# Moving where activation slots and weight tiles begin in SBUF: slots of 4096 bytes at multiples of 512, weights 320 bytes behind one

## The chip, the cores and the metric

One core of a Trainium2 chip. The metric is the device time of one execution in microseconds, the median of several runs; a profile of one further execution shows where its time lies.

## The reference, cut to what matters

Two model blocks follow one another on 256 tokens of width 1024, two layers each, all in float32. A layer of the first block has three attention branches (latent, differential, memory), a gated merge and a feed-forward part; a layer of the second has a state-space branch, a gated recurrence, an mLSTM branch, a merge and a convolved feed-forward part. Most of the work is products with weight matrices:

```python
u = _rmsnorm(h, norm_mix_g[l])
... = _split(u @ w_in[l], IN_SIZES_2)
y_ml = _mlstm_branch(m_q, m_k, m_v, m_i, m_f, m_o, ...)
merged = gate[0] * (y_ssd @ w_br_ssd[l]) + gate[1] * (y_hg @ w_br_hg[l]) + gate[2] * (y_ml @ w_br_ml[l])
h = h + merged @ w_out[l]
up = _dwconv(u @ w_up[l], ffn_conv_w[l], ffn_conv_b[l])
```

In the mLSTM branch the chunk scores are multiplied by the values `v` of each of 8 heads, and by a column of ones, which gives the normalizer.

## The kernel before, in words

**Products.** Each float32 factor is split into a high part of type fp32r and the rest, and a product is three matmuls: high weight by high activation, high weight by low activation, low weight by high activation (`mm` at line 230 issues all of them). `dense_b` (line 238) keeps weights stationary, 128 by 128, and streams 256 tokens of an activation; for each of nk blocks of 128 channels it issues the three, so an output tile is a chain of 3 nk matmuls. `dense_a` (line 262) keeps activations stationary and streams up to 512 columns of weights. `unit` (line 193) brings weights: a DMA of 512 KB into `raw`, a cast to `wh` on ScalarE (line 211), the rest to `wl` on VectorE (line 212). There are 4 `raw`, 6 `wh` and 6 `wl` tiles of 4096 bytes per partition, in pool `wgt`.

**Activations.** `slot` (line 114) hands out one of 24 tiles of `SLOT` = 1040 float32, 4160 bytes, from pool `big`; a block of 128 channels by 256 tokens is 1024 bytes of one. `pair` gives an activation as slots of high parts and slots of low parts, four channel blocks to a slot. Small things live in pools `const` (parameters, tables), `mid` (tiles of 2048 bytes and less, tagged) and `tiny` (32 tiles of 128 bytes).

**Addresses.** Pools lie behind one another in the order in which they are opened (`const`, `wgt`, `big`, `mid`, `tiny`, lines 93 to 97), the first at byte 16512 of each partition; a tile takes its bytes rounded up to 32. By the program's list of tiles the 16 weight tiles begin at 26048, 30144 and so on to 87488, all 448 bytes behind a multiple of 512. The 24 slots begin at 91584 + 4160 s, so slot s lies 448 + 64 s behind one, modulo 512: every multiple of 64 occurs, three times each. Blocks within a tile are steps of 512 or 1024 bytes, so a read has its tile's remainder. Below, the **distance** of an activation is its slot's remainder less the weights' 448, modulo 512. By the same list the activations of the stretches that the prediction reads have these:

| stretch, us | product | distances of high and low parts; after the semicolon those of the other four blocks |
|---|---|---|
| 36 to 50 | `w_in`, first 640 columns, layer 0 | 448 and 384; 64 and 0 |
| 374 to 455 | `mlp_w1`, layer 0 | 0 and 448; 320 and 64 |
| 894 to 966 | `mlp_w1`, layer 1 | 64 and 320; 384 and 256 |
| 1299 to 1327 | `w_br_ssd_2`, layer 0 | 448 and 192; 448 and 448 |
| 1650 to 1726 | `w_up_2`, layer 0 | 64 and 448; 320 and 192 |
| 2244 to 2270 | `w_br_hg_2`, layer 1 | 192 and 192; 0 and 448 |
| 2328 to 2349 | `w_out_2`, layer 1 (stationary) | 192 and 192; 448 and 0 |
| 2356 to 2480 | `w_up_2`, layer 1 | 192 and 64; 256 and 384 |

**Order of the work.** One program order per engine, made by the tile framework from the order of calls; `mix` (line 295) interleaves a stream of products ("main") with a branch's steps ("side") at a given rate, and `high_priority` draws weight loads forward. `ml_cols` (line 1127) takes slots for queries, keys and `va`, the values of four heads and two token halves with a column of ones behind each 128 (2 x 4 x 130 = 1040 floats, the reason for the size of a slot); `dense_a` fills it with one copy per token half; `mlstm` (line 1165) streams `va[:, s, i, :129]` for head i.

Of the kernel before, what the change touches and what calls it, by code (L numbers as in the profile page):

```python
# [9 lines left out]
F32 = mybir.dt.float32  # L10
# [9 lines left out]
P = 128  # L20
# [6 lines left out]
ALPHA = (2 * DEPTH) ** 0.25  # L27
THETA = 500000.0
BIG = 1e30
SLOT = 1040  # L30
AHEAD = 100
DEC = 4
MIX = (1.5, 0.5, 1.3, 1.2, 1.3, 0.9)
# [52 lines left out]
class Kern:  # L86
    def __init__(self, ctx, tc, a, out, dbg=None):
        self.tc, self.nc, self.a, self.out = tc, tc.nc, a, out
        self.dbg = dbg or {}
        nc = tc.nc  # L90
        self.V, self.A, self.T, self.G = nc.vector, nc.scalar, nc.tensor, nc.gpsimd
        pool = lambda n, b, **k: ctx.enter_context(tc.tile_pool(name=n, bufs=b, **k))
        self.pc = pool("const", 1)
        self.pw = pool("wgt", 2)
        self.pb = pool("big", 1)
        self.pm = pool("mid", 2)
        self.pt = pool("tiny", 4)
        self.nslot = 24
        self.fence = []
        self.early = []  # L100
        self.spare, self.turn = True, 0
        self.par = {}
        self.pd = pool("rowd", 1, space=bass.MemoryType.DRAM)
        self.ps = pool("ps", 4, space=PSUM)
        self.evn = 0
        self.nid = 0
        self.consts()
# [31 lines left out]
    def s2(self, shape, dt=F32, bufs=7, tag="s2"):  # L139
        if tag == "s2" and self.spare:  # L140

            self.turn += 1
            if self.turn * DEC // 12 != (self.turn - 1) * DEC // 12:
                return self.shape(self.pm.tile([P, 768], dt, tag="dec", name=self.nm(tag), bufs=DEC), shape)
        n = 512 if tag == "s2" else int(np.prod(shape))
        t = self.pm.tile([P, n], dt, tag=tag, name=self.nm(tag), bufs=bufs)
        return self.shape(t, shape)

    def tiny(self, shape, dt=F32):
        t = self.pt.tile([P, 32], dt, tag="tiny", name=self.nm("tiny"), bufs=32)  # L150
        return self.shape(t, shape)

    def psum(self, tag, shape, bufs):
# [224 lines left out]
    def params(self, vecs, tag):  # L378

        rows = sum(int(np.prod(v.shape)) // P for v in vecs)  # L380
        assert rows <= P
        r = self.pc.tile([P, P], F32, tag="prow", name=self.nm("prow"), bufs=1)
        o, offs = 0, []
        for v in vecs:
            n = int(np.prod(v.shape)) // P
            self.nc.sync.dma_start(out=r[o:o + n], in_=v.rearrange("(n p) -> n p", p=P))
            offs.append((o, n))
            o += n
        ps = self.ptp((P,))
        self.tr(out=ps[:, :rows], in_=r[:rows], identity=self.ident[:rows, :rows])  # L390
        c = self.pc.tile([P, P], F32, tag="pcol" + tag, name=self.nm("pcol"), bufs=2)
        self.V.tensor_copy(out=c[:, :rows], in_=ps[:, :rows])
        return [c[:, o:o + n] for o, n in offs]

# [160 lines left out]
    def first_layer(self, l, x, xT, last, filler):  # L555
        nc, V, A, T, a = self.nc, self.V, self.A, self.T, self.a
        w = a["w_in"][l]
# [12 lines left out]
            V.tensor_tensor(out=lt[:, 2 * i], in0=lt[:, 2 * i], in1=lt[:, 2 * i + 1], op=MUL)  # L570
            V.reduce_sum(out=lr[:, i:i + 1], in_=lt[:, 2 * i], axis=AX.X)
        A.activation(out=lr, in_=lr, func=AF.Exp)
        nlam = self.pc.tile([P, 1], F32, tag="nlam", name=self.nm("nlam"), bufs=2)
        V.tensor_tensor(out=nlam, in0=lr[:, 1:2], in1=lr[:, 0:1], op=SUB)
        V.tensor_scalar(out=nlam, in0=nlam, scalar1=-lam0, scalar2=None, op0=ADD)

# [4 lines left out]
        for i, (k0, k1) in enumerate(((0, 3), (3, 5))):  # L581
# [3 lines left out]
            for tt in range(2):  # L585
                for k in range(k0, k1):
                    self.mm(out=pss[:, 2 * i + tt:2 * i + tt + 1], lhsT=sq[k - k0][:, tt * P:(tt + 1) * P],
                             rhs=self.ones[:, :1], start=k == k0, stop=k == k1 - 1)
        rs = self.pc.tile([P, 4], F32, tag="lrs", name=self.nm("lrs"), bufs=2)
        self.rsqrt(rs[:, :2], pss[:, :2], 1.0 / 384, EPS)  # L590
        self.rsqrt(rs[:, 2:], pss[:, 2:], 1.0 / 256, EPS)
        cq, ck = self.pair(3), self.pair(2)
# [191 lines left out]
        if last:  # L784
            ms = self.s2((2, 2), tag="ms", bufs=2)
# [124 lines left out]
    def second_params(self, l):  # L910
        nc, V, A, a = self.nc, self.V, self.A, self.a
        lb = None
        flat = lambda v: v.rearrange("a b -> (a b)")
        nmix, cw, cbias, sng, hng, mng, nffn = self.params(
            [a["norm_mix_g_2"][l], flat(a["ssd_conv_w_2"][l]), a["ssd_conv_b_2"][l], a["ssd_norm_g_2"][l],
             a["hg_norm_g_2"][l], a["ml_norm_g_2"][l], a["norm_ffn_g_2"][l]], "a")
        fw = a["ffn_conv_w_2"][l]
        cols = [fw[0], fw[1]] + ([flat(a["hg_lb_raw_2"][i]) for i in range(DEPTH)] if l else [])
        f0, f1, *lbr = self.params(cols, "b")
        f2, fb = self.params([fw[2], a["ffn_conv_b_2"][l]], "c")  # L920
        sb = self.pc.tile([P, 96], F32, tag="sbias", name=self.nm("sbias"), bufs=2)
        for o, v in ((0, flat(a["ssd_dt_bias_2"][l])), (32, flat(a["ml_f_bias_2"][l])), (48, flat(a["ml_i_bias_2"][l])),
                     (64, flat(a["ssd_a_log_2"][l]))):
            n = v.shape[0]
            nc.sync.dma_start(out=sb[:, o:o + n], in_=v.rearrange("(o n) -> o n", o=1).broadcast_to([P, n]))
        dsk = self.pc.tile([P, 8], F32, tag="dsk", name=self.nm("dsk"), bufs=2)
        dv_ = a["ssd_d_2"][l].rearrange("(k two) -> two k", two=2)
        for i in range(2):
            nc.sync.dma_start(out=dsk[i * 64:(i + 1) * 64], in_=dv_[i:i + 1].broadcast_to([64, 8]), allow_slow_non_contiguous=True)
        V.tensor_scalar(out=dsk, in0=dsk, scalar1=0.5, scalar2=None, op0=MUL)  # L930
        for g_, c_ in ((sng, 0.5), (hng, 0.25), (mng, 0.5)):
            V.tensor_scalar(out=g_, in0=g_, scalar1=c_, scalar2=None, op0=MUL)
        if l:

            lb = self.pc.tile([P, 4, 16], F32, tag="lb", name=self.nm("lb"), bufs=2)
            mx, e0, e1 = (self.tiny((16,)) for _ in range(3))
            V.tensor_tensor(out=mx, in0=lbr[0], in1=lbr[1], op=MAX)
            for e_, r_ in ((e0, lbr[0]), (e1, lbr[1])):
                V.tensor_tensor(out=e_, in0=r_, in1=mx, op=SUB)
                A.activation(out=e_, in_=e_, func=AF.Exp)  # L940
            V.tensor_tensor(out=mx, in0=e0, in1=e1, op=ADD)
            V.reciprocal(out=mx, in_=mx)
            V.tensor_tensor(out=e0, in0=e0, in1=mx, op=MUL)
            V.tensor_tensor(out=e1, in0=e1, in1=mx, op=MUL)
            V.tensor_tensor(out=e1, in0=e0, in1=e1, op=ADD)
            V.tensor_tensor(out=lb[:, 0], in0=e1, in1=e0, op=SUB)
            V.tensor_scalar(out=lb[:, 1], in0=lb[:, 0], scalar1=-1.0, scalar2=1.0, op0=MUL, op1=ADD)
            V.tensor_scalar(out=lb[:, 2], in0=lb[:, 0], scalar1=0.5, scalar2=0.5, op0=MUL, op1=ADD)
            V.tensor_scalar(out=lb[:, 3], in0=lb[:, 1], scalar1=0.5, scalar2=None, op0=MUL)
        return nmix, cw, cbias, sng, hng, mng, nffn, f0, f1, f2, fb, sb, dsk, lb  # L950

    def second_layer(self, l, h, ms, rest):
        nc, V, A, a = self.nc, self.V, self.A, self.a
        w = a["w_in_2"][l]
        nmix, cw, cbias, sng, hng, mng, nffn, f0, f1, f2, fb, sb, dsk, lb = self.par[l]

        uT = self.rms_ch(h, ms, nmix, rest)
# [19 lines left out]
        ps = self.ptp((2, 64))  # L977
# [20 lines left out]
        dt = self.s2((2, 32), tag="dt", bufs=1)  # L998
# [128 lines left out]
        def ml_cols(hg):  # L1127
            o = 512 * hg
            q, k = self.slot((4, S)), self.slot((4, S))
            va = self.slot((2, 4, 130))  # L1130
            V.memset(va[:, :, :, 128:129], 1.0)
            def gen():
                yield from self.dense_b(uT, w[:, 7712 + o:7712 + o + 512], lambda j, m, ps: self.copy(q[:, j:j + m], ps))
                yield from self.dense_b(uT, w[:, 8736 + o:8736 + o + 512],
                                        lambda j, m, ps: A.mul(out=k[:, j:j + m], in_=ps, mul=128 ** -0.5))
                yield from self.dense_a(uT, [w[:, 9760 + o:9760 + o + 512]],
                                        lambda ci, tt, ps: self.copy(va[:, tt, :, :P], ps.rearrange("p (a b) -> p a b", b=P)))
            return (q, k, va), gen()
        def ml_gate(hg):
            o = 512 * hg  # L1140
# [24 lines left out]
        def mlstm(hg, rows, q, k, va, mo, out):  # L1165
            rd, atok, em = rows
            hs = self.slot((2, 4, P))
            sums = self.s2((2, 2, 4), tag="sums", bufs=2)
            def head(i):
# [9 lines left out]
                for tt in range(2):  # L1179
                    ps = self.ppo((2, 129))  # L1180
                    f = [(e[:, 0, tt * P:(tt + 1) * P], 0)] + ([(e[:, 1, S:], 1)] if tt else [])
                    b = [(e[:, 1, tt * P:(tt + 1) * P], 1)] + ([] if tt else [(e[:, 0, S:], 0)])
                    for d, ops in enumerate((f, b)):
                        for n, (lh, s) in enumerate(ops):
                            self.mm(out=ps[:, d], lhsT=lh, rhs=va[:, s, i, :129], start=n == 0, stop=n == len(ops) - 1)
                    den = self.tiny((2,))
                    A.activation(out=den, in_=ps[:, :, 128], func=AF.Abs)
                    V.tensor_tensor(out=den, in0=den, in1=em[:, tt, :, hd], op=MAX)
# [1 line left out]
                    o = hs[:, tt, i]  # L1190
# [4 lines left out]
            out = out()  # L1195
# [313 lines left out]
```

## Time and profile before

| | us |
|---|---|
| median of 3 runs | 2580.66 |
| the runs | 2576.44, 2580.66, 2670.82 |
| the profiled execution | 2577.26 |
| its span, first to last instruction | 2575.5 |

The runs are whole executions. All rows below belong to the profiled one, whose times run from its span's start. PE is TensorE's matmuls, PEld its weight loads, DVE is VectorE, ACT ScalarE, POOL GpSimd. A matmul's end is modelled and matmuls overlap, so the time of one in a row (0.28 us) is longer than the time from its start to the next one's.

### The profile page before, as it was taken

The numbers are of one execution on the slowest core, as the hardware profiler recorded it, in microseconds if no ns is written. First come the engines' busy times: TensorE is split into PE (matmuls) and PEld (weight loads), VectorE is DVE, ScalarE is ACT, GpSimd is POOL, SyncE is SP. The second block draws the span as 40 slices with busy tenths as digits, with TensorE's granted clock in tenths as the row PEclk, the third lists the DMA queues.
The fourth block names the chain that finished last, engine by engine and source line by source line (L and its number), as shares of the span: only waits on it lengthen the run. The fifth ranks groups of instructions, "written<-read, shape, count | busy, mean of one in ns | idle before, by whom it ended". The sixth has DMA issues, their size and how long they took to land. (4 is left out here: it accounts for less than half of the span.)

```text
span 2575.5 us, 50287 instructions
## 1 busy us (share of the span) xinstructions
PE 2503.5 (97%) x20432; PEld 2294.5 (89%) x20432; DVE 1846.5 (72%) x3229; ACT 1347.5 (52%) x2249; POOL 119.0 (5%) x175
## 2 busy tenths in 40 slices
PE   8999999999999999899899999999999999999998
PEld 8888999888889898798899998998898989998996
DVE  5577686566776865786678877985786689768875
ACT  5455455344654553465654445664556645445653
POOL 0000000000000000013300000000104200000000
PEclk9999999999999999899999999999999999999999
DMA  6643466556434565466564455655567554455653
GB/s 201 198 125 104 148 201 192 190 167 199 127 103 153 173 197 202 137 211 191 165 185 133 134 155 161 205 188 176 165 188 223 156 158 129 147 160 177 188 185 118
DMA packets 352424, 432.37 MB, mean 168 GB/s; under 512 B 21923, under 2 KB 279231, under 8 KB 352191
## 3 DMA queue, kind: packets, MB, share of 16 engines
q1 hardware_dynamic: 347838, 410.12, 51.4%
q0 software_dynamic: 4352, 19.03, 2.4%
q8 instruction: 161, 2.64, 0.4%
q14 instruction: 73, 0.59, 0.1%
HBM read 427.89 MB, written 1.20 MB: 167 GB/s over the span
## 5 line engine op out<-in xcount | busy, mean ns | idle before, releaser
L230 PE MATMUL mm<-s,wh 128*128 128x256 f32 (+1 forms) x8064 | 1464.5, 284 | 1.6 <-DVE s L521 0.7
L230 PEld LDWEIGHTS mm<-s,wh 128*128 128x128 f32 (+1 forms) x8064 | 1242.6, 189 | 19.2 <-issue 13.1
L212 DVE TENSOR_TENSOR wl<-raw,wh 128x1024 fp32r<-128x1024 f32 (+1 forms) x776 | 933.8, 1211 | 436.1 <-ACT wh L211 431.4
L211 ACT CAST wh<-raw 128x1024 fp32r<-128x1024 f32 (+1 forms) x776 | 799.0, 1039 | 770.4 <-PE mm L230 672.5
L230 PE MATMUL mm<-s,wl 128*128 128x256 f32 x4032 | 1136.7, 282 | 0.0
L230 PEld LDWEIGHTS mm<-s,wl 128*128 128x128 f32 x4032 | 761.3, 189 | 3.1 <-issue 2.7
L230 PE MATMUL mm<-wh,s 128*128 128x512 f32 (+2 forms) x2160 | 673.4, 393 | 11.8 <-DVE s L520 6.6
L230 PEld LDWEIGHTS mm<-wh,s 128*128 128x128 f32 x2160 | 406.2, 191 | 102.5 <-DVE s L520 8.4
L230 PE MATMUL mm<-wl,s 128*128 128x512 f32 (+2 forms) x1080 | 421.4, 390 | 0.0
L230 PEld LDWEIGHTS mm<-wl,s 128*128 128x128 f32 x1080 | 206.5, 191 | 43.0
L230 PE MATMUL tp<-s,s 128*32 128x16 f32 (+5 forms) x3552 | 120.7, 208 | 6.7 <-issue 4.5
L233 PE MATMUL tp<-cst,s 128*128 128x128 f32 (+1 forms) x608 | 93.2, 284 | 21.8 <-DVE s L825 6.4
L907 ACT ACTIVATE dec<-dec,rtok 128x256 f32<-128x256 f32 x192 | 73.3, 447 | 74.3 <-POOL dec L903 66.9
L853 DVE SCALAR_TENSOR_TENSOR s<-mm,pcol,s 128x255 f32<-128x255 f32 (+1 forms) x272 | 112.0, 473 | 0.0
L230 PEld LDWEIGHTS tp<-s,s 128*32 128x32 f32 (+3 forms) x3552 | 91.0, 119 | 23.5 <-issue 7.9
L233 PEld LDWEIGHTS tp<-cst,s 128*128 128x128 f32 (+1 forms) x608 | 70.8, 142 | 37.3 <-issue 10.1
L893 POOL DMA_DIRECT2D rds<-rows x8 | 4.1, 518 | 1627.6 <-DVE rows L876 1627.6
L455 ACT ACTIVATE s<-tp,tiny 128x256 f32<-128x256 f32 x112 | 52.1, 471 | 51.7 <-DVE tiny L452 44.9
L1406 DVE TENSOR_TENSOR s<-s,s 128x512 f32<-128x512 f32 x112 | 71.9, 685 | 9.3 <-PE tp L230 8.8
L335 ACT CAST s<-s 128x512 fp32r<-128x512 f32 x46 | 28.3, 619 | 57.3 <-DVE s L765 37.4
L1057 DVE TENSOR_TENSOR dec<-dec,s 128x768 f32<-128x768 f32 x32 | 32.4, 1016 | 35.3 <-ACT dec L907 24.4
L230 PE MATMUL po<-s,s 128*128 128x128 f32 (+2 forms) x352 | 54.0, 311 | 1.1 <-DVE s L344 0.8
(237 smaller groups left out, 1591.1 us busy)
## 6 DMA issues: line engine op xcount, KB each, us to landing
raw<-in_w_in_dram SPq DMA_DIRECT2D x338, 512.0 KB
raw<-in_mlp_w_dram SPq DMA_DIRECT2D x128, 512.0 KB
raw<-in_w_up_dram SPq DMA_DIRECT2D x88, 512.0 KB
raw<-in_w_down_dram SPq DMA_DIRECT2D x44, 512.0 KB
raw<-in_w_branch_dram SPq DMA_DIRECT2D x32, 512.0 KB
raw<-in_w_out_dram SPq DMA_DIRECT2D x32, 512.0 KB
dec<-rds POOLq DMA_DIRECT2D x32, 384.0 KB, 5.4
raw<-in_mem_w_kv_dram SPq DMA_DIRECT2D x16, 512.0 KB
```

Of the source, the lines that this page charges most:

```text
L211: i.append(self.A.copy(out=h, in_=raw))
L212: i.append(self.V.tensor_tensor(out=l, in0=raw, in1=h.bitcast(F32), op=SUB))
L230: return self.T.matmul(**k)
L233: return self.T.transpose(**k)
L335: return (self.A.copy(out=xh, in_=src), self.V.tensor_tensor(out=xl, in0=src, in1=xh.bitcast(F32), op=SUB))
L455: self.A.activation(out=e[:, i], in_=sc[:, i], func=AF.Exp, bias=mx[:, i:i + 1], scale=scale, accum_out=sm[:, i:i + 1])
L853: V.scalar_tensor_tensor(out=o, in0=x, scalar=w[i][c + d], in1=o, op0=MUL, op1=ADD)
L893: self.nc.gpsimd.dma_start(out=d[:, s, c], in_=src)
L907: self.A.activation(out=e[:, s, o], in_=e[:, s, o], func=AF.Exp, scale=-1.0, bias=tok[:, s, q:q + 1])
L1057: V.tensor_tensor(out=e, in0=e, in1=cb[hd // 8], op=MUL)
L1406: V.tensor_tensor(out=xv, in0=xv, in1=tv[:, :, tside].unsqueeze(2).to_broadcast([P, 2 * m, L]), op=MUL)
```

## The change

The pools are opened in another order and a new one, `small`, comes first; `gap` comes between the weights and the slots, and `const` behind the slots. `nlam`, `lrs` and `dsk` move to `small`, `ms` and `sums` to `gap`. A slot has 1024 floats. The values of the mLSTM branch no longer fit one: heads 0 to 2 take a slot, head 3 a tile of tag `va` in pool `mid`, filled by two copies per token half where there was one, and the column of ones by two memsets. To pay for that, `tiny` has 31 tiles and one parameter tile 96 columns.

```diff
-SLOT = 1040
+SLOT = 1024
@@
+        self.pa = pool("small", 1)
+        self.pw = pool("wgt", 2)
+        self.pg = pool("gap", 1)
+        self.pb = pool("big", 1)
         self.pc = pool("const", 1)
-        self.pw = pool("wgt", 2)
-        self.pb = pool("big", 1)
         self.pm = pool("mid", 2)
@@ def s2
-        t = self.pm.tile([P, n], dt, tag=tag, name=self.nm(tag), bufs=bufs)
+        t = (self.pg if tag in ("ms", "sums") else self.pm).tile([P, n], dt, tag=tag, name=self.nm(tag), bufs=bufs)
@@ def tiny
-        t = self.pt.tile([P, 32], dt, tag="tiny", name=self.nm("tiny"), bufs=32)
+        t = self.pt.tile([P, 32], dt, tag="tiny", name=self.nm("tiny"), bufs=31)
@@ def params
-        c = self.pc.tile([P, P], F32, tag="pcol" + tag, ...)
+        c = self.pc.tile([P, 96 if tag == "c" else P], F32, tag="pcol" + tag, ...)
@@ nlam, lrs and dsk, two tiles each
-        nlam = self.pc.tile([P, 1], ...)
+        nlam = self.pa.tile([P, 1], ...)
@@ def ml_cols
-            va = self.slot((2, 4, 130))
-            V.memset(va[:, :, :, 128:129], 1.0)
+            va = self.slot((2, 3, 130)), self.s2((2, 1, 130), tag="va", bufs=2)
+            for t in va:
+                V.memset(t[:, :, :, 128:129], 1.0)
+            def ev_v(ci, tt, ps):
+                ps = ps.rearrange("p (a b) -> p a b", b=P)
+                self.copy(va[0][:, tt, :, :P], ps[:, :3])
+                self.copy(va[1][:, tt, :, :P], ps[:, 3:])
@@
-                                        lambda ci, tt, ps: self.copy(va[:, tt, :, :P], ...))
+                yield from self.dense_a(uT, [w[:, 9760 + o:9760 + o + 512]], ev_v)
@@ def mlstm
-                            self.mm(out=ps[:, d], lhsT=lh, rhs=va[:, s, i, :129], ...)
+                            self.mm(out=ps[:, d], lhsT=lh, rhs=va[i // 3][:, s, i % 3, :129], ...)
```

## Rows read from the trace of the kernel before

**Rows 1.** The page: busy time of two engines; the granted clock in 40 slices.

```profile
PE 2503.5 (97%) x20432; PEld 2294.5 (89%) x20432; DVE 1846.5 (72%) x3229; ACT 1347.5 (52%) x2249; POOL 119.0 (5%) x175
...
PEclk9999999999999999899999999999999999999999
```

**Rows 2.** Matmuls grouped by shape: count, busy us and mean ns, idle before.

```profile
L230 PE MATMUL mm<-s,wh 128*128 128x256 f32 x8032 | 1458.9, 284 | 1.6 <-DVE s L521 0.7 <-DVE s L520 0.6
L230 PE MATMUL mm<-s,wl 128*128 128x256 f32 x4016 | 1132.2, 282 | 0.0
L230 PE MATMUL mm<-wh,s 128*128 128x512 f32 x1984 | 632.9, 399 | 9.5 <-DVE s L520 6.6 <-DVE s L521 1.4 <-ACT wh L211 1.3
L230 PE MATMUL mm<-wl,s 128*128 128x512 f32 x992 | 393.3, 396 | 0.0
```

**Rows 3.** Timeline in `mlp_w1`, layer 0: start us, length us, engine, line, operation, count.

```profile
371.02 0.28 PE L230 MATMUL mm<-s,wh 128*128 128x256 f32 x1
371.02 0.19 PEld L230 LDWEIGHTS mm<-s,wl 128*128 128x128 f32 x1
```

**Rows 4.** Windows of `dense_b` alone, PE: length us, busy us (matmuls), clock, DMA.

```profile
36.50:50.30 13.80, 13.80 (x118) 1.00 0.41 121
893.70:966.20 72.50, 72.50 (x618) 1.00 0.65 202
1650.50:1726.40 75.90, 75.90 (x646) 1.00 0.59 190
2356.00:2480.00 124.00, 124.00 (x1051) 1.00 0.62 195
374.00:455.00 81.00, 81.00 (x702) 1.00 0.66 208
1299.50:1310.00 10.50, 10.50 (x95) 1.00 0.48 147
```

**Rows 5.** Timeline of `w_br_hg_2`, layer 1, on PE, columns as in rows 3.

```profile
2246.06 0.40 PE L230 MATMUL mm<-s,wh 128*128 128x256 f32 x2
...
2247.13 0.40 PE L230 MATMUL mm<-s,wh 128*128 128x256 f32 x2
...
2247.48 0.40 PE L230 MATMUL mm<-s,wh 128*128 128x256 f32 x2
...
2247.83 0.39 PE L230 MATMUL mm<-s,wh 128*128 128x256 f32 x2
...
2248.85 0.40 PE L230 MATMUL mm<-s,wh 128*128 128x256 f32 x2
```

**Rows 6.** Timeline of `w_br_ssd_2`, layer 0, on PE, 1321.8 to 1324.

```profile
1321.82 0.40 PE L230 MATMUL mm<-s,wh 128*128 128x256 f32 x2
...
1323.94 0.28 PE L230 MATMUL mm<-s,wh 128*128 128x256 f32 x1
```

**Rows 7.** Windows of `dense_a` alone, PE, columns as in rows 4.

```profile
467.00:547.90 80.90, 80.90 (x350) 1.00 0.57 185
966.50:1055.00 88.50, 88.50 (x384) 1.00 0.58 188
2327.90:2349.50 21.60, 21.60 (x96) 1.00 0.53 167
```

**Rows 8.** What PE waited for: us in total, times, longest.

```profile
PE tp L230 <- POOL s L1095: 9.4, 4, 3.6
PE mm L230 <- DVE s L520: 7.2, 8, 1.5
...
PE mm L230 <- ACT wh L211: 1.3, 1, 1.3
```

**Rows 9.** Window with the busiest VectorE: PE, PEld, DVE, ACT, POOL, clock, DMA.

```profile
1600.00:1700.00 100.00, 99.37 (x838) 98.69 (x837) 88.91 (x150) 66.10 (x100) 0.00 (x0) 1.00 0.61 191
```

**Rows 10.** Copies of 512 columns from a product's PSUM tile, by engine and shape.

```profile
L344 DVE COPY s<-mm 128x512 f32<-128x512 f32 x26 | 17.8, 686 | 6.1 <-PE mm L230 6.1
...
L346 ACT COPY s<-mm 128x512 f32<-128x512 f32 x26 | 15.1, 582 | 8.4 <-PE mm L230 8.4
```

More of the change, by code (lines that the diff above doesn't have):

```diff
@@ L390, in params @@
         self.tr(out=ps[:, :rows], in_=r[:rows], identity=self.ident[:rows, :rows])
-        c = self.pc.tile([P, P], F32, tag="pcol" + tag, name=self.nm("pcol"), bufs=2)
+        c = self.pc.tile([P, 96 if tag == "c" else P], F32, tag="pcol" + tag, name=self.nm("pcol"), bufs=2)
         self.V.tensor_copy(out=c[:, :rows], in_=ps[:, :rows])
@@ L572, in first_layer @@
         A.activation(out=lr, in_=lr, func=AF.Exp)
-        nlam = self.pc.tile([P, 1], F32, tag="nlam", name=self.nm("nlam"), bufs=2)
+        nlam = self.pa.tile([P, 1], F32, tag="nlam", name=self.nm("nlam"), bufs=2)
         V.tensor_tensor(out=nlam, in0=lr[:, 1:2], in1=lr[:, 0:1], op=SUB)
@@ L588, in first_layer @@
                              rhs=self.ones[:, :1], start=k == k0, stop=k == k1 - 1)
-        rs = self.pc.tile([P, 4], F32, tag="lrs", name=self.nm("lrs"), bufs=2)
+        rs = self.pa.tile([P, 4], F32, tag="lrs", name=self.nm("lrs"), bufs=2)
         self.rsqrt(rs[:, :2], pss[:, :2], 1.0 / 384, EPS)
@@ L925, in second_params @@
             nc.sync.dma_start(out=sb[:, o:o + n], in_=v.rearrange("(o n) -> o n", o=1).broadcast_to([P, n]))
-        dsk = self.pc.tile([P, 8], F32, tag="dsk", name=self.nm("dsk"), bufs=2)
+        dsk = self.pa.tile([P, 8], F32, tag="dsk", name=self.nm("dsk"), bufs=2)
         dv_ = a["ssd_d_2"][l].rearrange("(k two) -> two k", two=2)
@@ L1135, in gen @@
                                         lambda j, m, ps: A.mul(out=k[:, j:j + m], in_=ps, mul=128 ** -0.5))
-                yield from self.dense_a(uT, [w[:, 9760 + o:9760 + o + 512]],
-                                        lambda ci, tt, ps: self.copy(va[:, tt, :, :P], ps.rearrange("p (a b) -> p a b", b=P)))
+                yield from self.dense_a(uT, [w[:, 9760 + o:9760 + o + 512]], ev_v)
             return (q, k, va), gen()
@@ L1184, in head @@
                         for n, (lh, s) in enumerate(ops):
-                            self.mm(out=ps[:, d], lhsT=lh, rhs=va[:, s, i, :129], start=n == 0, stop=n == len(ops) - 1)
+                            self.mm(out=ps[:, d], lhsT=lh, rhs=va[i // 3][:, s, i % 3, :129], start=n == 0, stop=n == len(ops) - 1)
                     den = self.tiny((2,))
```

## The prediction

> **What bounds the kernel now.** First the page: TensorE is busy 97% of the span and its clock is granted in full (2.4 GHz) but for one slice, VectorE 72%, ScalarE 52% [rows 1]. Then who waits: 61 waits of PE in 21 lines, 61.1 us in all, the largest on GpSimd's sum of squares and on the splits that end a norm; on a cast of weights 1.3 us [rows 8]. So the kernel is a stream of matmuls, and the question is how far apart they start. By shape, 12,048 of the 20,432 are 256-column matmuls of `dense_b` and 2,976 are 512-column ones of `dense_a` [rows 2]. While one streams its moving operand, the weight load of the next already runs: both rows begin at 371.02 [rows 3]. The means of rows 2 are modelled and overlap, so spacing is read elsewhere.
>
> In a window of nothing but such matmuls the spacing is its length over the count, less the 2.4 that were in flight at its start (0.28 us each, one every 0.118). That gives 72.5/615.6 = 117.8 ns in `mlp_w1` of layer 1, 75.9/643.6 = 117.9 and 124/1048.6 = 118.3 in the two `w_up`, but 81/699.6 = 115.8 in `mlp_w1` of layer 0 and 10.5/92.6 = 113.4 in `w_br_ssd` of layer 0 [rows 4]. Same shape, same clock; the DMA shares of 0.48 to 0.66 don't order them (0.59 goes with 117.9, 0.66 with 115.8). What does is the table of distances between slots and weight tiles. At 113.4 every slot lies 192 or 448 behind the weights, the same modulo 256. In layer 0's `mlp_w1` half of the blocks (320 and 64, the same modulo 256 again) run at 113.5 in 31 chains and the other half (0 and 448) at 117.7: mean 115.6. Mixed distances stay at 117.5 or more: 117.8 and even in `w_up` of layer 0, where all are odd multiples of 64, and 13.8/115.6 = 119.4 in the slowest window, with 384 beside 448.
>
> The change puts weights at 320 and slots at 0: every distance becomes 192. That case stands in the trace: in `w_br_hg` of layer 1 the first four blocks have 192 and 192, the last 0 and 448. From 2246.06 to 2247.13, nine starts in the last four, (2247.13 - 2246.06)/9 = 119 ns; in the next chain, after an entry of three matmuls, (2248.85 - 2247.83)/9 = 113.3 [rows 5]. All eight half chains of this kind there, three of them after a stall of 0.3 us, settle so within five matmuls (entry gaps 122, 116, 114).
>
> But distance alone doesn't decide. In the same `w_br_ssd` product, after some microseconds at the 1.2 GHz level and back, the same slots run at (1323.94 - 1321.82)/18 = 117.8 [rows 6]. So there are two steady spacings, 113.4 and 117.8, and how a stretch is entered chooses.
>
> **The change part by part.** All is summed against the profiled execution, 2577.26 us (span 2575.5), 3.4 us under the median of the runs.
>
> *Addresses.* Three pairs of small tiles of 32 bytes move `wgt` to 16512 + 192 = 16704 = 32 x 512 + 320. Its 16 tiles of 4096 end at 82240; `ms` (2 x 32) and `sums` (2 x 64) make 82432 = 161 x 512, where slots begin, each a multiple of 512. The distance is 0 - 320 = 192 everywhere.
>
> *`dense_b`.* Of its 12,096 matmuls (48 have 64 columns) 11,707 start less than 140 ns before the next, on average 117.8; the rest follow a stall, another shape or the half clock and keep their time. The stretch of 1299.5 to 1310 with its entry gives 113.6. Gain at full effect: 4.2 x 11,707 = 49 us.
>
> *`dense_a`.* Here weights move and slots are stationary. In flight are 1.7; 80.9/348.3 = 232.3 and 88.5/382.3 = 231.5 with mixed slots, 21.6/94.3 = 229.1 in `w_out` of layer 1, half of whose blocks have 192 [rows 7]. I take 231.5 to 229.0, 2.5 x 2,877 undisturbed = 7 us; the bounds are the slowest window, 232.3 (2 us lost), and the same gain once more, 226.5 (14 us), since only half of that stretch had the new distance.
>
> *What takes some back.* 61 waits of PE [rows 8] end with work of other engines that doesn't hurry. A wait grows by what PE gains since that work was released: at most about a unit of 48 matmuls, 48 x 4.2 = 0.2 us, 12 us for all, 0 where PE's own result was awaited; I take 5. VectorE at its busiest has 88.9 of 100 us [rows 9], 92 at the new pace, no bound. Weights come at up to 202 GB/s in rows 4 and would at 210.
>
> *The state.* Chains at 192 alone went short in 8 of 8 cases; the long state of rows 6 came out of a half-clock stretch, and the page shows few of these. I count a tenth of `dense_b` at 117.8: 5 us; the bounds are none (0) and all (49).
>
> *Values of the mLSTM.* Two layers, two head groups, two token halves: 8 copies of 512 columns become 16, of 384 and 128. A copy costs 0.69 us on VectorE, 0.58 on ScalarE [rows 10]; the added one costs at least nothing, if halves run side by side on two engines, and at most a whole one, 8 x 0.69 = 5.5 us, beside products of 24 x 2 matmuls that last 11 us. I take 0 on the path; without that cover, 3. Four more memsets of 8 columns, parts of a tenth of a microsecond each: 0. One `tiny` fewer of 32 can delay a writer by one reader; no wait in rows 8's view is for such a slot: 0, bound 1. Behind a delayed VectorE write would stand the weight splits, which run ahead by up to six tiles. Tables that only move keep shape and engine: 0; no row shows an address that slows VectorE or ScalarE, and I allow 1 us either way. No DMA is added or moved, and `raw` keeps its shape.
>
> Sum: -49 - 7 + 5 + 5 = -46, so 2577 - 46 = **2531 us**. That is 1.9% under the median, close to the 2% that a measurement of this kernel can tell from no change.
>
> **Against a rule.** Rows 4 to 6 show equal matmuls at two spacings. The Trainium skill ("TensorE: Matmul & The Clock Gate", Part 2, on loading the stationary operand) says that moving operand and weight load have read ports of their own, so that loading the next weights takes nothing from the running matmul. By it addresses can't matter and the time would be 2577; this trace doesn't agree, 113.4 against 117.8 ns. It is a rival below for the part that the trace leaves open.
>
> **The rivals.**
> 1. *All short (0.27).* As above without the long tenth, and waits that grow by 1 or 2 us alone: 2577 - 49 - 7 + 2 = 2523, with 226.5 in `dense_a` 2516. For it: 8 of 8. Against: rows 6. It is faster by over 2% from 2529 down.
> 2. *The long spacing keeps most (0.15).* The state of rows 6 is taken at an entry and kept: `dense_b` 117.8, `dense_a` gains 0 to 7: 2570 to 2577. Half of it as a mixture would be 2548. For: rows 6, and `mlp_w1` of layer 1, where the half at 64 and 320 ran at 117.8 too. Against: those were other distances, but for rows 6. The rule above gives the same time by another way.
> 3. *Slower (0.05).* Slots are now 4096 apart, so high and low parts agree in twelve bits of their address, as no pair before did. If reads of the two in turn collide, the spacing is that of the slowest window, 119.4 [rows 4]: 1.6 x 11,707 = 19, with 2 of `dense_a` 2598. It decides from a mean spacing above 118; over 2% (2632) it takes 122.5, which no window shows.
> 4. *It doesn't do what it says (0.02).* If pools begin at larger steps, distances are equal but another number: 2520 to 2590.
>
> **How the numbers follow.** The forecast, mostly short, has 0.51, its own range 2522 to 2545. Rival 1 has 0.27, 2 has 0.15, 3 has 0.05, 4 has 0.02. The range 2514 to 2574 holds all of the first two, and half of rival 2. Faster by over 2%: rival 1 and a fifth of the forecast, 0.27 + 0.10 = 0.37; slower by over 2%: a fifth of rival 3 and as much for what isn't listed, 0.02; within 2%: 0.61.
>
> **What would show it.** Windows inside `w_up` and `mlp_w1` with 113.4 between starts (75.9 us for 646 matmuls becomes 73), `dense_a` at 229, and PE's waits nearly as long as now. It is wrong if flat 117.8 stands in `w_up`, if the short stretches are there and the waits of PE have grown by 20 us or more, or if spacings differ where all distances are one.

## The result and the profile after

The changed kernel takes 2548.95 us (median of four runs, 2536.19 to 2550.88), the kernel before 2578.55 beside it; the ratio on record is 0.9873, 95% interval 0.9851 to 0.9895 (the two medians alone give 0.9885). One run of the kernel before, 2670.82 us, is a slow one, 3.7% over its fastest, and doesn't count in the ratio. The forecast was 2531 with a range of 2514 to 2574. Measured twice more, unedited, the changed kernel gave 0.9899 [0.9879, 0.9919] and 0.9866 [0.9850, 0.9883]. The gain is 1.0 to 1.3%; by the three pairs of medians it is 24 to 33 us, half to 70% of the 46 us that were forecast. The profiled run took 2536.19 us and is the shortest of all; where a reading hangs on that, other profiles of the same kernel stand beside it.

Busy time and clock of the page, and the two shapes of `dense_b`, which answer to [rows 1, 2] (lines of the kernel after lie some four higher):

```profile
PE 2455.7 (97%) x20432; PEld 2253.2 (89%) x20432; DVE 1850.5 (73%) x3237; ACT 1348.5 (53%) x2253; POOL 117.2 (5%) x175
...
PEclk9999999999999999899999999999999999999999
```

```profile
L234 PE MATMUL mm<-s,wh 128*128 128x256 f32 x8032 | 1418.9, 280 | 2.0 <-DVE s L525 0.7 <-DVE s L524 0.5 <-DVE s L857 0.3
L234 PE MATMUL mm<-s,wl 128*128 128x256 f32 x4016 | 1119.3, 279 | 0.0
```

PE has the same 20,432 matmuls and is as full as before; it only takes 48 us less for them. VectorE and ScalarE have their added instructions (8 and 4) and nearly their old times. So the change lies in the spacing of the matmuls. Windows of nothing but `dense_b`, columns as in [rows 4], in order: the 640-column product of layer 0, `mlp_w1` of layers 0 and 1, `w_up` of layer 0 before and behind the loading of parameters, `w_up` of layer 1:

```profile
37.00:50.80 13.80, 13.80 (x119) 1.00 0.43 121
357.90:449.50 91.60, 91.60 (x811) 1.00 0.62 193
882.70:952.40 69.70, 69.70 (x618) 1.00 0.67 208
1581.20:1626.00 44.80, 44.80 (x383) 1.00 0.68 208
1629.40:1702.40 73.00, 73.00 (x646) 1.00 0.64 196
2319.80:2438.90 119.10, 119.10 (x1053) 1.00 0.66 202
```

Less the 2.4 in flight, that is 118.4, 113.3, 113.2, 117.7, 113.4 and 113.4 ns. `mlp_w1` of layer 1 and both large `w_up` stood at 117.8 to 118.3 before. Every distance is now 192, and still the first and the fourth window are at the long spacing. Below, a stretch at 113.4 is called short and one at 117.8 long; this state is its spacing alone. From the starts of all matmuls in the trace: stretches without an interruption run flat at 113.4 or at 117.8, never between, and a stretch keeps its spacing to its end. That the two are one product is seen in `w_up` of layer 0, where one small transpose changes the state (timeline, columns as in [rows 3]):

```profile
1626.93 0.40 PE L234 MATMUL mm<-s,wh 128*128 128x256 f32 x2
...
1628.70 0.40 PE L234 MATMUL mm<-s,wh 128*128 128x256 f32 x2
...
1629.06 0.24 PE L237 MATMUL tp<-cst,prow 88*128 88x88 f32 x1
```

Ahead of it fifteen starts take (1628.70 - 1626.93)/15 = 118 ns; behind it the window of 1629.4 to 1702.4 above has 113.4, with the same tiles and addresses. In all four profiles of the unedited kernel the state changes at this transpose, in three from long to short and in one the other way. In the kernel moved on by 64 bytes, below, it doesn't: both sides are long.

`dense_a`, 231.5 to 232.3 ns in [rows 7], in the product behind `mlp_w1` of layer 0:

```profile
450.00:541.00 91.00, 91.00 (x399) 1.00 0.59 186
```

Less the 1.7 in flight that is 91/397.3 = 229.0 ns. The mean over all undisturbed `dense_b` matmuls (starts less than 140 ns apart) went from 117.82 to 114.59 ns, of `dense_a` from 231.53 to 229.15: 3.2 x 11,725 = 38 and 2.4 x 2,871 = 7 us. With 5 us more waits of PE (61.1 to 66.3 in sum) that is -40; the two profiled executions differ by 41. The other three profiles of the changed kernel took 2552 to 2557 us; what sets them apart comes below.

### The profile page after: what moved, and what is told of

Same layout as the page of the kernel before. It is cut to its first block, busy times and chain, and to the rows that moved or that the text cites. A ratio compares the mean times of both kernels' runs of the same rounds, so it can differ in the third digit from the quotient of the medians.

```text
span 2533.5 us, 50296 instructions
## 1 busy us (share of the span) xinstructions
PE 2455.7 (97%) x20432; PEld 2253.2 (89%) x20432; DVE 1850.5 (73%) x3237; ACT 1348.5 (53%) x2253; POOL 117.2 (5%) x175
## 5 line engine op out<-in xcount | busy, mean ns | idle before, releaser
L234 PE MATMUL mm<-s,wh 128*128 128x256 f32 (+1 forms) x8064 | 1424.6, 280 | 2.0 <-DVE s L525 0.7
L234 PEld LDWEIGHTS mm<-s,wh 128*128 128x128 f32 (+1 forms) x8064 | 1228.6, 188 | 19.2 <-issue 11.4
L234 PE MATMUL mm<-s,wl 128*128 128x256 f32 x4032 | 1123.8, 279 | 0.0
```

The lines of the kernel that those rows point to most:

```text
L234: return self.T.matmul(**k)
```

## The experiments

Two theories stand at the start. R: the relation of slot and weight addresses allows two spacings, and the state at entry picks one. M: it is the slots' beginning at multiples of 512 that counts. S is the rival by which addresses don't matter and the gain comes from the order of the pools or the split of the values. The Trainium skill ("TensorE: Matmul & The Clock Gate", Part 2), with a read port each for moving operand and weight load, speaks for it. The runs below don't agree (in the kernel 119.9 ns at distance 0 against 114.6 at 192). The first three experiments on the kernel are one execution each, with one of the kernel before beside them (2573.62 us).

### The same distance at other addresses

```
+        self.pa.tile([P, 16], F32, name="pad_small")
         self.pc = pool("const", 1)
```

> Every tile behind the small ones is moved on by 64 bytes: weights 384, slots 64 behind a multiple of 512, distance still 192. Theory R: as the changed kernel, 2531 to 2552 us, the long `w_up` and `mlp_w1` stretches flat at 113.4 ns in most cases. Theory M: slots are no longer at multiples of 512, so 117.8 ns and 2570 to 2580 us. Theory S: 2531 to 2552 us, since pool order and split stay.

Measured: 2549.29 us. Windows in `mlp_w1` of layer 1 and the two `w_up`:

```profile
887.80:960.30 72.50, 72.50 (x618) 1.00 0.68 208
1633.30:1709.20 75.90, 75.90 (x647) 1.00 0.63 190
2333.30:2452.40 119.10, 119.10 (x1053) 1.00 0.66 202
```

Slots at 64 behind a multiple of 512 give the same two spacings: 113.4 in the last window, 117.8 in the first two, which were short in the kernel after. M falls. R's "in most cases" is a miss: `mlp_w1` of both layers and `w_up` of layer 0 behind its transpose are long, and by the mean of 115.16 ns 39% of all `dense_b` matmuls. The state isn't settled by the distance.

### Distance 0 at multiples of 512

```
+        self.pa.tile([P, 48], F32, name="pad_small")
+        self.pg.tile([P, 80], F32, name="pad_gap")
         self.pc = pool("const", 1)
```

(and three of the `tiny` buffers fewer, to make room)

> Weights and slots both begin at multiples of 512, distance 0 everywhere. Theory R: distance 0 gave 117.7 ns in the kernel before (half of `mlp_w1` of layer 0, with 448 beside it), so nearly all of `dense_b` at 117.8 ns and 2570 to 2585 us. Theory M: slots are at multiples of 512, so as the changed kernel, 2531 to 2552 us. Theory S: 2531 to 2552 us.

Measured: 2592.32 us, 19 over the kernel before. Windows in `mlp_w1` of layer 1, in both `w_up`, and in `dense_a`:

```profile
896.30:970.10 73.80, 73.80 (x617) 1.00 0.63 196
1658.10:1735.40 77.30, 77.30 (x647) 1.00 0.60 187
2369.90:2496.10 126.20, 126.20 (x1054) 1.00 0.63 192
974.00:1057.00 83.00, 83.00 (x368) 1.00 0.62 195
```

73.8/614.6 = 120.1 ns in `dense_b`, flat in every stretch (mean 119.87); 83/366.3 = 226.6 in `dense_a`. This falsifies M and S at once: rounder addresses made the kernel slower. It also corrects R, which had expected 117.8. Distance 0 has a spacing of its own, over the mean of every long mixed stretch, and the shortest seen for `dense_a`.

### Mixed distances with the rest of the change

```
-        t = self.pb.tile([P, SLOT], dt, tag="s4", ...
+        t = self.pb.tile([P, SLOT + 16], dt, tag="s4", ...
```

(and twelve `tiny` buffers fewer)

> The changed kernel with slots 4160 bytes apart, so that all eight remainders occur again; weights stay at 320, the values of the mLSTM stay split and the pools keep the new order. Theory R: `dense_b` back at 117.5 to 118 ns, `dense_a` at 231 to 232, 2572 to 2582 us. Theory M: one slot in eight is at a multiple of 512: 2570 to 2580 us. Theory S: the gain stays, 2531 to 2552 us.

Measured: 2580.95 us, `dense_b` at 118.07 and `dense_a` at 231.55 in the mean. The same four places:

```profile
897.10:969.90 72.80, 72.80 (x618) 1.00 0.64 196
1653.80:1729.60 75.80, 75.80 (x646) 1.00 0.61 189
2360.00:2483.80 123.80, 123.80 (x1054) 1.00 0.63 195
588.50:643.70 55.20, 55.20 (x240) 1.00 0.66 198
```

The whole gain is gone. Of the 7 us over the kernel before, 0.25 x 11,700 = 3 are the spacing, and the rest lies within the spread of that kernel's own runs (2573.62 to 2582.81). PE's waits are 63.6 us in sum, against 61.1 before, so the fewer `tiny` buffers hide no gain of size. The split of the mLSTM's values and the new order of the pools bring nothing on their own. S falls.

### The spacing by itself

```
    for d in DIST:                    # 29 distances
        for r in range(6):
            part(1 + r)               # 1 to 6 fp32 matmuls, two passes each
            for i in range(4):
                chain(d, i % 2)       # 12 matmuls: wh,xh  wh,xl  wl,xh
```

> Nothing but matmuls of the two kinds: for each of 29 distances between slots and weights, six chains of 48 `dense_b`-like matmuls (256 columns, a high and a low slot, a high and a low weight tile, in the kernel's order), each entered through one to six fp32 matmuls; then, for 16 distances, three times 24 `dense_a`-like matmuls of 512 columns. The reference's computation is left out. Theory R (the relation of the two addresses and the state at entry set the spacing): the steady spacing is 113.4 or 117.8 ns, at distances 192 and 448 113.4 in most of the six entries, at mixed ones 117.8, and which entries give 117.8 differs with the number of matmuls ahead. Theory M (slots at multiples of 512 bytes decide, whatever the weights): 117.8 at every distance but where slots lie at a multiple of 512, distance 384 here. Theory S (addresses don't matter, the gain came from the pool order and the split of the values): one spacing at all 29 distances.

Windows of single chains of 48: distance 0, then 32, then the first two entries at 192.

```profile
39.50:45.10 5.60, 5.60 (x49) 1.00 0.00 0
57.80:63.30 5.50, 5.50 (x49) 1.00 0.01 3
239.20:244.70 5.50, 5.50 (x49) 1.00 0.01 3
245.30:250.60 5.30, 5.30 (x49) 1.00 0.00 0
```

The same 49 matmuls fill 5.3 us in one entry and 5.5 in the one before it, with next to no DMA and with VectorE and ScalarE idle. The ends of a window cost some tenths of a matmul, so the table is taken from the starts, matmul 7 to 48 of each chain (7 to 24 for 512 columns):

```
distance   256 columns, ns (by entry)    512 columns, ns
0          120.0                         226.7 (some start at 230.8)
32         116.7                         233.3
64         117.8                         233.3
96         120.0                         234.2 to 234.5
128        118.6                         232.3
160        117.3 or 118.6                233.3
192        113.3 or 117.8 (3 of 6 each)  228.8
224        118.3                         233.4
```

256 to 480 repeat this row by row: only the remainder modulo 256 counts. (At 640 and 896, which are like 128, two of the six entries gave 120.0.) R was right at 192 and 448, and too simple elsewhere: not one long spacing, but one or two for each distance. 192, with its like 448, is the only one of these 16 with a spacing under 116; finer steps, below, find another.

### High and low tiles at different remainders, and what picks the state

```
    for d1, d2, e in GRID:      # xh from wh: d1; xl from wl: d2; xl and wl moved on by e
    for n, c, d in SEP:         # n leads of c columns at distance d, then distance 192
```

> Again nothing but matmuls, the reference's computation left out. First chains of 24 `dense_b`-like matmuls over an 8 x 8 table of two distances, of the high slot from the weights that load while it streams, and of the low slot from those that load while it streams, each entered after 2, 4 and 6 passes of fp32; then finer distances around 192, and distance 192 with low slot and low weights moved on together by 32, 64 or 128 bytes. Theory R in its sharper form (each matmul is held up by the weight load of the next one, and only the distance of these two counts): moving both low tiles together changes nothing, 113.3 or 117.8 ns; the diagonal of the table repeats the 29 distances measured before, 0 at 120.0, 32 at 116.7, 192 at 113.3 or 117.8; no pair is under 113.3. Rival: the absolute address counts too, and moving both gives a third spacing. Then distance 192 with one to four extra matmuls ahead of the chain, of another distance or another number of columns: if the state is a phase between the two reads, some of these ends at 113.3 in all six entries; if it is chance, each of them gives about half.

With low slot and low weights moved on together by 32, 64 or 128 bytes every matmul still sees distance 192 from the weights that load meanwhile, and yet the steady spacing is 119.1, 118.4 and 120.9. The sharper form of R falls: where the low tiles begin against the high ones counts as well. In the table of pairs only 192 with 192 reached 113.3 in more than one entry (two of three); one entry at 64 with 64 did too. None is under 113.3. Among the finer distances, 112 has a mean of 114.3 to 114.5 in its three entries (matmul 9 to 24), which the next section takes apart. Of the leads, one of 128 columns at distance 192 and one of 256 at distance 0 or 32 gave 113.3 in six of six entries; without one it was three of six.

### Fifteen ways in

```
    for sep in SEP:                 # none, or a lead
        for kind, n in PRE:         # 15 entries
            pre(kind, n)
            chain2(sep)             # distance 192
```

> Nothing but matmuls, the reference's computation left out. Chains at distance 192 entered in 15 ways (1 to 3 fp32 matmuls of 128, 256 or 64 columns, a 512-column product, a wait for VectorE of four lengths), each plain and with seven leads: a 128-column matmul ahead of the first one (it gave 113.3 in six of six entries before), the first matmul in two halves of 128 columns, in 64 and 192, in 192 and 64, and 128 or 256 columns at another distance. Phase theory (the state is the phase between two periodic reads at entry, so a lead that shifts one of them by a fixed amount picks it): the plain chains split between 113.3 and 117.8, one or two leads give 113.3 in at least 13 of 15. Chance theory: every lead gives about as many as the plain chains. Then distances 96 to 152 in steps of 4, from the 114.4 ns that 112 gave in three of three entries: if 112 is no accident, 108 to 116 lie between 113 and 118, and some distance needs no luck at entry; its 512-column matmuls are 229 to 234.

```
lead ahead of the chain             113.3 ns in, of 15
none                                8
128 columns                         15
256 columns, distance 32            15
first matmul as 128 + 128           14
256 columns, distance 0             13
first matmul as 64 + 192            13
first matmul as 192 + 64            7
128 columns, distance 32            5
```

Not chance: what starts just ahead of the chain picks the state. And 112 is no accident: its mean is 114.2 to 114.5 in four of four entries too, while 108 and 116 have 120 and 122. This mean is no spacing of its own. The first entry, three starts from row to row:

```profile
62.43 0.28 PE L47 MATMUL mm<-sh,wl 128*128 128x256 f32 x1
...
63.49 0.28 PE L47 MATMUL mm<-sh,wl 128*128 128x256 f32 x1
...
64.85 0.28 PE L47 MATMUL mm<-sh,wl 128*128 128x256 f32 x1
```

Nine starts take 1.06 us, 117.8 ns; the twelve behind them 1.36 us, 113.3. So it went in all seven entries at 112, four here and three in the study before: about ten matmuls at 118 to 119, then 113.3 to the end of the 24. At 192 no plain chain left the long state. So 112 may need no luck at entry, as the expectation asked; how it holds over a long stretch wasn't run. Its price is `dense_a`: 512 columns take 233 there against 229 at 192.

### The changed kernel again

> The changed kernel once more, unedited. Theory R: its stretches are flat at 113.4 or 117.8 ns again, but not the same ones as in the first profile; each 4.4 ns x matmuls of the stretches that flip make up the difference of the two times, which is 2536 to 2551 us. Rival (the place in the program sets the state): the same stretches at the same spacing, and a difference of times that comes from waits.

Measured: 2556.41 us, beyond what R had. The mean spacing is 114.72, nearly that of the first profile, and all stretches over 400 matmuls are short in both. States do flip, as R had it: some 2,300 of 11,600 matmuls, short to long for 1,350 and the other way for 980. But that nearly cancels: 0.13 ns x 11,700 = 1.5 of the 20 us between these two runs. The rest is the rival's waits, with the clock beside them. Where they arise is seen by laying the same matmuls of both side by side. Six places are together 19.9 us longer; two of them (columns: length; busy time of PE, PEld, DVE, ACT, POOL; clock; DMA), first profile:

```profile
1209.10:1235.90 26.80, 24.68 (x203) 22.45 (x202) 21.33 (x24) 20.48 (x44) 12.78 (x17) 1.00 0.77 226
...
1944.40:1970.20 25.80, 24.04 (x204) 21.43 (x201) 19.80 (x19) 22.40 (x48) 15.92 (x21) 1.00 0.81 246
```

and again:

```profile
1209.60:1240.40 30.80, 26.85 (x203) 24.04 (x201) 20.53 (x24) 21.10 (x45) 14.05 (x19) 0.89 0.67 204
...
1953.60:1984.90 31.30, 26.96 (x205) 23.69 (x202) 18.92 (x20) 23.19 (x48) 17.60 (x22) 0.89 0.67 204
```

The same work takes 4.0 and 5.5 us longer: part of it ran at the 1.2 GHz level, and PE idles more (2.1 and 1.8 us before, 4.0 and 4.3 now). Both lie in stages in which GpSimd works beside the products (12.8 to 17.6 us busy). The waits of PE there (us in total, times, longest; before, first profile, again):

```profile
PE po L230 <- DVE dec L1057: 6.0, 6, 1.8
...
PE po L234 <- DVE dec L1061: 3.9, 6, 1.2
...
PE po L234 <- DVE dec L1061: 8.3, 6, 2.1
```

In the second profile the granted clock fell to 1.2 GHz at 1218.6 and 1966.1 us, each time behind a wait for `dec` (1.94 and 2.12 us). In the first profile the same two waits were 1.18 us and the clock stayed. The kernel before has both falls, at 1235.1 and 1986.0 us. So the first profile, 2536 us, was a lucky one.

### Leads in the kernel

```
+                    if (self.nid, i) in self.LEAD:
+                        self.mm(out=ps[:, i, :P], lhsT=h[:, 0, o:o + P], rhs=xh[:, 0, :P], start=True, stop=True)
```

> The changed kernel with one more matmul of 128 columns ahead of a chain in each of the 30 `dense_b` stretches of 84 matmuls and more, at the start of the stretch or up to 24 matmuls into it; its sum is overwritten. Phase theory: behind the lead every one of these stretches is flat at 113.4 ns, none at 117.8; it costs 30 x 0.1 = 3 us and gives back 4.4 ns x the matmuls that were long, 6 us against the first profile of the changed kernel, 13 us against the one shifted by 64 bytes: 2530 to 2545 us, 0.982 to 0.987 of before, 0 to 10 us under the changed kernel in the same call. Chance theory: a third of the 30 stay at 117.8, and the time is that of the changed kernel or 3 us over it.

> The changed kernel unedited, beside the one with leads. Phase theory: 2536 to 2557 us, a quarter to two fifths of `dense_b` long; what differs from the other two profiles beyond 4.4 ns x the long matmuls stands in stretches at the half clock of the GLA and mLSTM stages.

Measured: with 30 leads 2566.13 us, 0.9955 of before [0.9937, 0.9972]; unedited, beside it, 2551.99, 0.9899 [0.9879, 0.9919]. The leads cost 14 us, where a gain was expected, and the trace says why. `mlp_w1` of layer 0, where the lead falls into a running stretch:

```profile
363.22 0.28 PE L234 MATMUL mm<-s,wl 128*128 128x256 f32 x1
...
364.58 0.28 PE L234 MATMUL mm<-s,wl 128*128 128x256 f32 x1
364.69 0.51 PE L234 MATMUL mm<-s,wh 128*128 128x128 f32 x3
365.04 0.28 PE L234 MATMUL mm<-s,wl 128*128 128x256 f32 x1
...
366.10 0.28 PE L234 MATMUL mm<-s,wl 128*128 128x256 f32 x1
```

Between rows of `wl` lie three starts. Ahead of the lead 1.36 us for twelve, 113.3 ns; behind it 1.06 for nine, 117.8, and so for the 790 matmuls that follow. It was the same in all eight stretches of 214 and more that a lead cut into: every one short ahead of it and long behind it. The sum agrees: 1.0 ns more on 11,700 matmuls and 30 x 0.1 us are 15 us. Of the twelve leads at the start of a stretch, eight gave the short state. In all, 21 of the 30 were long behind their lead, so both expectations are missed (none, or a third). A lead behind another kind of work tends to give the short state, and one inside the short state ended it. That fits a phase that an odd matmul shifts; the phase itself is in no trace. `dense_b` came to 115.97 in the mean, against 114.98 unedited.

In this third profile of the unedited kernel (2557.11 us) the large `w_up` stretches of layer 0 and layer 1 are long, as 35% of `dense_b` is:

```profile
1630.50:1706.30 75.80, 75.80 (x646) 1.00 0.61 191
2336.30:2460.10 123.80, 123.80 (x1053) 1.00 0.64 194
```

So large stretches do flip between runs of one kernel: 4.7 us by the second window alone.

### Leads at the starts alone

> The changed kernel with the lead at nine of the 30 places alone: those where it stands at the start of the stretch (in one case after three matmuls), the stretch was at 117.8 in at least one profile without a lead, and at 113.4 in the profile with 30 leads. None stands in a running stretch. Phase theory: these nine (118, 118, 94, 94, 381, 94, 94, 121 and 1053 matmuls) are at 113.4 ns; without leads they were long for 832 matmuls in the first profile and 1,558 in the third, so 3 to 6 us go and 9 x 0.1 come: 2 to 6 us under the changed kernel of the same call. Chance theory: about a third of the nine are long, and the times are the same.

> The changed kernel unedited, for the interval beside the one with nine leads: 2540 to 2556 us, 0.987 to 0.991 of before.

Measured: 2545.40 us, 0.9873 [0.9858, 0.9887], and unedited 2544.79, 0.9866 [0.9850, 0.9883]: no difference. Eight of the nine stretches are at 113.4, two of them here in the first rows; the ninth and largest, `w_up` of layer 1, is long:

```profile
36.80:50.00 13.20, 13.20 (x119) 1.00 0.46 134
1578.30:1621.30 43.00, 43.00 (x382) 1.00 0.70 214
2326.90:2450.70 123.80, 123.80 (x1053) 1.00 0.63 195
```

There the lead was in a place where it can't act (timeline, in brackets the idle time before and what ended it):

```profile
2325.38 0.22 PE L234 MATMUL mm<-s,wh 128*128 128x128 f32 x1
2325.87 0.38 PE L234 MATMUL mm<-s,wh 128*128 128x256 f32 x1 [0.26 <-DVE s L528]
2326.59 0.39 PE L234 MATMUL mm<-s,wh 128*128 128x256 f32 x1 [0.34 <-DVE s L529]
```

Behind the lead PE waits twice for the halves of the split, so the stretch is entered anew. The stretch of 382 has such waits behind its lead too and came out short, and so did `w_up` of layer 1 with 30 leads: there the lead shows nothing. The seven others are short, and were chosen for having been so with 30 leads; in the unedited profile beside them (2551.93 us) five of these seven are long, 545 matmuls. What that gives, 4.4 ns x 545 = 2.4 us, is less than the 4.7 us that the large stretch lost. (By the states of their matmuls, six of the nine stretches were long in the first profile, 926 matmuls, and four in the third, 1,362; the expectation has 832 and 1,558.) A lead behind these waits, in another PSUM bank, was not tried. No version beat the changed kernel by what can be measured.

## Why the prediction came out as it did

- *Two spacings, 113.4 and 117.8, chosen at entry and kept: right.* It was read from a table of distances and two short timelines [rows 4 to 6], and holds in all profiles with distance 192. What decides an entry, left open then, is what PE runs just ahead: so in the study, and in the kernel as far as the leads show it.
- *Distance 192 for the short one: right*, and not at round addresses (distance 0: 119.9, slower than before). In the study, of all multiples of 32 only 192 and its like modulo 256 reach 113.3 often; 112 reached it in all seven entries. At 64, which the prediction read as a short distance in `mlp_w1` of layer 0 (113.5), 24 entries of the study gave 117.8 and one of three in the table of pairs 113.3.
- *`dense_a`, 231.5 to 229.0: right*, 229.15 to 229.54 in four profiles. The bound of "the same gain once more" (226.5) belongs to distance 0, where `dense_b` loses more.
- *The tenth at the long spacing: the term of the sum that was mis-sized.* Reckoned as (mean - 113.45)/4.33, 26, 29, 35 and 29% of `dense_b` was long in four profiles of the unedited kernel, 13 to 18 us instead of 5. "8 of 8" came from half chains in one product, all entered in much the same way; with entries of other kinds it is 8 of 15 in the study. By this two of the prediction's own signs of being wrong came true: flat 117.8 stands in `w_up` (382 matmuls of layer 0), and spacings differ where all distances are one.
- *The waits: mis-sized as well.* I took 5 us with 12 as a bound; PE's waits went from 61.1 to 66.3, 76.6, 75.7 and 74.6, so 5 to 16, against one profile of before (the kernels with distance 0 and with mixed distances, at the long spacing, have 64.5 and 63.6). The bound held a wait to grow by what PE gains. It left out the clock, which fell behind some of the longer waits. The mean granted clock was 0.990 in the profile before, 0.992 in the first one after and 0.988 in the other three: in these a half-clock time of twice the missing share, 2 x 0.012 x 2554 = 61 us against 2 x 0.010 x 2575 = 51, and half of the difference, 5 us, is lost; in the first, 5 us are won. That a longer wait brings the clock down is read from the order of events, and no run tested it.
- *The split of the values at 0: consistent*, since the kernel with mixed distances that has it gains nothing and PE gets no new wait of size. The prediction's 202 GB/s for the weights was misread: [rows 4] hold 208 as well. It bounds nothing; a window with leads ran at 214.

With sizes from the means of the four profiles: -51 (`dense_b` all short, 4.37 x 11,700) -7 + 15 (long part) + 12 (waits) + 2 (clock) = -29, so 2548; the four profiled executions have a mean of 2550. The median of 2548.95 lies inside the stated range and 4 us above the forecast's own 2522 to 2545. Rival 2 named half a mixture as 2548. That it comes so near is luck: a quarter to a third was long, and waits made up the rest. Rival 3 was refuted as a mechanism: slots 4096 apart, high and low alike in twelve bits, run at 113.4. Slower spacings than before do exist, at distance 0 and with low tiles moved on against high ones (118.4 to 120.9), but whether reads collide there isn't shown. Why the distance acts as it does isn't settled: the runs show which addresses and entries give which spacing, not the wiring behind it.

## What to carry to other kernels

When TensorE is the bound, take the spacing from start to start of one shape in windows of nothing else; two values for equal matmuls at equal clock are worth a table of operand addresses. Lay out moving tiles and weight tiles so that all pairs, high and low, have the one distance that a short study of matmuls alone shows to be best: roundness is no guide, and mixed addresses hide that there is a choice. Look at the starts one by one: a mean over a chain can hide that it settles (112 here). For this kernel 112 is the next layout to try: an estimate from the study's spacings is 15 us less for the long part and 4 ns x 2,870 = 11 us more for `dense_a`. Count on part of the stretches taking the other state at 192, and on waits of PE to take back a share of what PE gains.

## What the runs showed of the hardware

- fp32r matmuls of 256 columns ran steadily at anything from 113.3 to 123.3 ns by the addresses of their operands and, at some distances, by what PE ran ahead, at full clock and with next to nothing else at work; those of 512 columns at 226.7 to 234.5. The best distances for the two shapes differ (192 or 112 for the first, 0 for the second).
- Four bytes matter: distance 196 gave 122 ns, 188 about 118, 192 113.3 or 117.8; 112 settled at 113.3 in seven of seven entries, between 120 and 122 at 108 and 116.
- A stretch of over a thousand matmuls keeps the spacing it was entered with, and a single matmul of 128 columns, or a transpose of 88, can change it for the rest: the first in 8 of 8 stretches of 214 and more, the second in four of four profiles of the unedited kernel.
- Moving a stretch of equal work from the short to the long state or back is the largest single difference between two runs of this kernel that isn't a wait or the clock: 4.7 us in one product.
